# Weight blocks of a feed-forward pair dealt out in strict turn, with places of their own for the small ones

## The chip, the cores and the metric

One core of a Trainium2 chip runs the kernel. The metric is device time in microseconds (us), from the start to the end of one execution.

## The reference

A decoder trunk of two layers on 256 tokens of width 2048, all in 32-bit floats. Layer 0 has sparse attention with chosen keys, layer 1 a sliding window over shared keys and values; each is followed by a SwiGLU feed-forward part and a gated embedding. The change concerns the feed-forward part alone:

```python
def swiglu(h, w1, w3, w2):
    return (jax.nn.silu(h @ w1) * (h @ w3)) @ w2
...
        x = x + swiglu(rmsnorm(x, g_ffn[i]), w1[i], w3[i], w2[i])   # w1, w3: 2048 x 5632, w2: 5632 x 2048
```

## The kernel before

**Products in three parts.** Every 32-bit operand is split into a rounded part `hi` and a rest `lo`. A product of a 128x128 activation tile (the stationary side, `st_hi` and `st_lo`) with a 128x512 weight tile is three multiplications on PE (L379 to L381): `hi` by `st_hi`, `lo` by `st_hi`, `hi` by `st_lo`. The activations are split once, the weights as they stream in.

**The weight stream** (`WeightStream`) walks one list of blocks. A full block holds four weight tiles (1 MB, 128x2048) and feeds 24 multiplications: 4 tiles, 2 halves of the tokens, 3 parts. For each, the SP queue loads a place `raw` (3 places), ACT makes `hi` (L123) and DVE makes `lo` (L124) in a pool with 3 places each. `next()` hands the next block to PE, and splits ahead so far that the block in use and the two behind it are split (`LOOK`). A `hi` can be made only when PE is done with the block that held the place three blocks before. ACT, DVE, PE and the SP queue each work strictly in their order; a scheduler writes that order when the program is built.

**A pair of chunks.** The feed-forward part works on 11 pairs in each layer, each a 512-wide chunk of `w1` and the same chunk of `w3`, in groups of 3, 4 and 4; after a group its rows of `w2` follow as full blocks. A pair is 256 tokens by 2048 by twice 512. For the first 4 of its 16 weight tiles (two of each kind: quadrants B11, B21 of `w1` and B12, B22 of `w3`) the kernel uses a Strassen-like scheme of 7 products in place of 8: sums of quadrants against sums of activation quadrants (`s_hi`, `s_lo`), into `side` accumulators or straight into the four outputs `acc0` to `acc3` (c11, c21, c12, c22). These 7 blocks are small: two tiles, 128x1024, and 6 multiplications each. DVE forms the sums in place (L118). The other 12 tiles of each chunk come as 3 full blocks per chunk. So a pair has 7 small and 6 full blocks, 42 + 144 = 186 multiplications.

The list of a pair's blocks before is: r11, r12, F, r11, r21, F, r11, r22, F, r11, F, F, F, where an F is a full block and r11 is split anew after each sum. A small block takes one of the three full-size places for `hi` and `lo`, and counts as one block of look-ahead.

**The end of a pair.** DVE adds the side products into v1, v6, v7, v8 (L477 to L480) and the accumulators (L604, L610); ACT makes the sigmoid (L606) and DVE the gate u (L607, L611). The gate is turned: two DVE transposes of 32x32 blocks (L312) into `xb`, then 16 copies on ACT (L317, moves=(1, 1)) into `xt`, then a split into the station `hid` (L299 on ACT, L300 on DVE), which the products with `w2` read after the group.

Of the kernel before, what the change touches and what calls it, by code (L numbers as in the profile page):

```python
# [12 lines left out]
F32 = mybir.dt.float32  # L13
F32R = mybir.dt.float32r
# [4 lines left out]
P = 128  # L19
# [51 lines left out]
class Block:  # L71

    def __init__(self, src, a, n, held=None, loads=(), sums=()):
        self.src, self.a, self.n, self.held, self.loads, self.sums = src, a, n, held, loads, sums


class WeightStream:
# [6 lines left out]
    def __init__(self, tc, raw_pool, half_pool, blocks):  # L86
        self.tc, self.nc, self.raw_pool, self.half_pool = tc, tc.nc, raw_pool, half_pool
        self.blocks = blocks
        self.held_pool = None
        self.loaded, self.halves, self.held = {}, {}, {}  # L90
        self.n_loaded = self.n_split = self.at = 0
        self.after = None

    def load(self, pool=None):
        i = self.n_loaded
        if i >= len(self.blocks):
            return
        b = self.blocks[i]
        self.n_loaded += 1
        for name, src in b.loads:  # L100
            self.held[name] = t = self.held_pool.tile([P, b.a * b.n], F32, tag=name, name=name, bufs=1)
            self.nc.sync.dma_start(t.rearrange("p (a n) -> p a n", a=b.a), src)
# [9 lines left out]
    def split(self):  # L112
        i = self.n_split
        if i >= len(self.blocks):
            return
        b = self.blocks[i]
        for o, p in b.sums:
            self.nc.vector.tensor_add(self.held[o], self.held[o], self.held[p])  # L118
        raw = self.loaded.pop(i) if b.held is None else self.held[b.held]
        hi = self.half_pool.tile([P, 4 * CW], F32R, tag="hi", name="hi")  # L120
        lo = self.half_pool.tile([P, 4 * CW], F32R, tag="lo", name="lo")
        m = b.a * b.n
        done = (self.nc.scalar.activation(hi[:, :m], raw[:, :m], AF.Copy),  # L123
                self.nc.vector.tensor_sub(lo[:, :m], raw[:, :m], hi[:, :m].bitcast(F32)))  # L124
# [4 lines left out]
        self.n_split += 1  # L129
# [13 lines left out]
def yoco_kernel(  # L143
# [22 lines left out]
    def pair_cols(wa, ca, wb, cb, nk):  # L166

        def at(w, k, c):
            return w[k * P:(k + SN) * P, c:c + CW].rearrange("(a p) n -> p a n", p=P)

        b11, b21, b12, b22 = at(wa, 0, ca), at(wa, SN, ca), at(wb, 0, cb), at(wb, SN, cb)
        rest = [cols(w, 2 * SN, nk - 2 * SN, c, CW) for w, c in ((wa, ca), (wb, cb))]
        def held(name, **more):
            return Block(None, SN, CW, held=name, **more)
# [130 lines left out]
    def transposed_blocks(pool, src, out=None, bufs=1, moves=(0, 1)):  # L305


        xb = pool.tile([P, 4, 4, NT, 32], F32, tag="xb", name="xb", bufs=bufs)
        xt = (pool.tile([P, 4, S], F32, tag="xt", name="xt", bufs=2) if out is None else out).rearrange(
            "p k (t q) -> p k t q", t=NT)  # L310
        for t in range(NT):
            nc.vector.transpose(out=xb[:, :, :, t, :], in_=src[t].rearrange("p (k j f) -> p j k f", k=4, j=4))  # L312
        for i in range(4):
            for j in range(4):
                o, s = xt[32 * j:32 * j + 32, :, :, 32 * i:32 * i + 32], xb[32 * i:32 * i + 32, j]
                if moves[(i + j) % 2]:
                    nc.scalar.activation(o, s, AF.Copy)  # L317
# [32 lines left out]
    def square_sum(ss, c, scratch):  # L350
        for t in range(NT):
            sq = (ps_tr.tile([P, CW], F32, tag="tr", name="sq") if scratch is None
                  else scratch.tile([P, CW], F32, tag="g", name="sq", bufs=2))
            nc.scalar.activation(sq, x[t][:, c * CW:(c + 1) * CW], AF.Square, accum_out=ss[:, t, c:c + 1])

    def rstd_of(ss, name):
# [23 lines left out]
        nc.tensor.matmul(o, sh, l, start=False, stop=False)  # L380
        return nc.tensor.matmul(o, sl, h, start=False, stop=last)  # L381

    def accumulate(st, ktiles, n, acc, pace=(), start=0, end=None, new=None):


        block = 0
# [1 line left out]
        while done < (len(ktiles) if end is None else end):  # L388
            hi, lo, a = stream.next()
            for j in range(a):  # L390
# [1 line left out]
                h, l = hi[:, j * n:(j + 1) * n], lo[:, j * n:(j + 1) * n]  # L392
                first, last = done + j == (0 if new is None else start), done + j == len(ktiles) - 1
                for t in range(NT):
                    end_ = products(st, acc[t][:, :n], kt, t, h, l, first and (new is None or new[t]), last)
            done += a
            work(pace[block] if block < len(pace) else 0)
            block += 1
# [47 lines left out]
    def pair_of_chunks(st, forms, nk, quad):  # L446
# [8 lines left out]
        def form(o, of, alone):  # L455
            hi, lo, a = stream.next()
            for j in range(a):
                sl = slice(j * CW, (j + 1) * CW)
                products_of(*of(j), o, hi[:, sl], lo[:, sl], alone != "more" and j == 0, alone == "alone" and j == a - 1)
# [21 lines left out]
        form(c12, forms.of(4), "first")  # L481
        accumulate(st, ktiles, CW, (c12, c22), (), 2 * SN, 2 * SN + 4, new=(False, True))
        form(c21, tiles(SN, 1), "more")
        accumulate(st, ktiles, CW, (c11, c21), (), 2 * SN + 8)
# [111 lines left out]
    def feed_forward(layer, st, forms, r, ss, nxt, scratch):  # L596
        for gi, (f0, f1) in enumerate(FGROUPS):
            hid = new_station()
            for f in range(f0, f1):
                quad = [ps_acc.tile([P, CW], F32, tag="acc", name=f"acc{j}") for j in range(4)]  # L600
                v = pair_of_chunks(st, forms, KT, quad)
                u = []
                for t in range(NT):
                    nc.vector.tensor_add(v[t], v[t], quad[t])  # L604
                    u.append(scratch.tile([P, CW], F32, tag="g", name="u", bufs=2))
                    nc.scalar.activation(u[t], v[t], AF.Sigmoid, scale=r[:, t:t + 1])  # L606
                    nc.vector.scalar_tensor_tensor(u[t], v[t], r[:, t:t + 1], u[t], op0=ALU.mult, op1=ALU.mult)  # L607
                accumulate(st, ALL, CW, quad[2:], (), 2 * SN + 4)
                for t in range(NT):
                    nc.vector.tensor_sub(v[2 + t], quad[2 + t], v[2 + t])  # L610
                    nc.vector.scalar_tensor_tensor(u[t], v[2 + t], r[:, t:t + 1], u[t], op0=ALU.mult, op1=ALU.mult)  # L611
                ut = transposed_blocks(scratch, u, moves=(1, 1))
# [56 lines left out]
    def embedding_end(st, pst, r, ss, halves, scratch, emb_pool, end):  # L669
# [14 lines left out]
        for t in range(NT):  # L684
            for s in range(2):
# [7 lines left out]
                sq = scratch.tile([P, CW], F32, tag="g", name="sq", bufs=2)  # L693
# [246 lines left out]
```

## Time and profile before

| what | us |
|---|---|
| runs of the kernel before: median (lowest to highest of 3) | 2344.95 (2343.69 to 2347.48) |
| the profiled execution: its time | 2347.13 |
| its span, first to last instruction | 2345.4 |
| PE, DVE, ACT busy in the span | 2235.3, 1631.5, 1302.4 |
| the 22 pairs of chunks together | 1081.61 |

The profile is one execution, 2347.13 us long, of which 2345.4 us are its span. PE means the matrix engine, DVE the vector engine, ACT the scalar engine, POOL is hardly used, and SP issues nearly all loads. A line such as L123 is one of the kernel; `hi<-raw` is what it writes and reads. Behind a bar or in square brackets stands how long the engine was idle before, and who ended that. One thing needs care: a multiplication's record is longer than the spacing at which PE starts them, so records overlap, and PE's busy share hides waits. Starts have to be compared with starts.

### The profile page before, as it was taken

The numbers are of one execution on the slowest core, as the hardware profiler recorded it, in microseconds if no ns is written. First come the engines' busy times: TensorE is split into PE (matmuls) and PEld (weight loads), VectorE is DVE, ScalarE is ACT, GpSimd is POOL, SyncE is SP. The second block draws the span as 40 slices with busy tenths as digits, with TensorE's granted clock in tenths as the row PEclk, the third lists the DMA queues.
The fourth block names the chain that finished last, engine by engine and source line by source line (L and its number), as shares of the span: only waits on it lengthen the run. The fifth ranks groups of instructions, "written<-read, shape, count | busy, mean of one in ns | idle before, by whom it ended". The sixth has DMA issues, their size and how long they took to land.

```text
span 2345.4 us, 25010 instructions
## 1 busy us (share of the span) xinstructions
PE 2235.3 (95%) x9780; PEld 1793.8 (76%) x9780; DVE 1631.5 (70%) x1728; ACT 1302.4 (56%) x1698; POOL 39.1 (2%) x38
## 2 busy tenths in 40 slices
PE   9999999999899999999999999999999999999998
PEld 8787877777677877788788777777777787777877
DVE  5877776756776477767787777776577656777755
ACT  5556655543655355566675667555355633565653
POOL 0111000000000000000000000000000000000000
PEclk9999999999999999999999999999999999999999
DMA  7554645555446554465565455556554565445553
GB/s 247 180 180 144 215 149 174 192 185 163 164 151 223 182 167 159 145 214 195 169 225 198 149 175 170 174 174 201 168 182 160 188 197 176 156 153 198 200 184 123
DMA packets 211383, 419.23 MB, mean 179 GB/s; under 512 B 7729, under 2 KB 14513, under 8 KB 211137
## 3 DMA queue, kind: packets, MB, share of 16 engines
q1 hardware_dynamic: 208400, 410.68, 52.7%
q0 software_dynamic: 1248, 4.27, 0.6%
q10 hardware_dynamic: 1616, 2.69, 0.3%
q8 instruction: 76, 1.25, 0.2%
q14 instruction: 43, 0.34, 0.0%
HBM read 415.48 MB, written 2.12 MB: 178 GB/s over the span
## 4 chain that ended last, share of the span: by engine, by line
PE 78%; ACT 10%; DVE 9%; issue 2%; ACTq 0%; POOLq 0%; DVEq 0%; POOL 0%
PE acc L380 25%; PE acc L381 25%; PE acc L379 24%; DVE lo L124 5%; ACT hi L123 5%; ACT xt L317 4%; PE ps_s L537 1%; PE ps_o L574 1%; DVE v L477 1%; DVE v L610 0%; DVE u L611 0%; PE ps_p L565 0%; PE side L381 0%; PE side L380 0%; DVE xb L312 0%
## 5 line engine op out<-in xcount | busy, mean ns | idle before, releaser
L379 PE MATMUL acc<-hi,st_hi 128*128 128x512 f32 (+2 forms) x2872 | 1112.8, 392 | 43.7 <-ACT hi L123 43.3
L380 PE MATMUL acc<-lo,st_hi 128*128 128x512 f32 (+2 forms) x2872 | 1120.0, 390 | 32.4 <-DVE lo L124 32.4
L381 PE MATMUL acc<-hi,st_lo 128*128 128x512 f32 (+2 forms) x2872 | 1113.5, 388 | 0.0
L124 DVE TENSOR_TENSOR lo<-raw,hi 128x2048 fp32r<-128x2048 f32 (+1 forms) x347 | 793.0, 2291 | 394.3 <-ACT hi L123 393.1
L123 ACT ACTIVATE hi<-raw 128x2048 fp32r<-128x2048 f32 (+1 forms) x347 | 655.8, 1897 | 734.9 <-PE acc L381 640.3
L379 PEld LDWEIGHTS acc<-hi,st_hi 128*128 128x128 f32 x2872 | 540.3, 189 | 176.7 <-ACT hi L123 69.0
L380 PEld LDWEIGHTS acc<-lo,st_hi 128*128 128x128 f32 x2872 | 543.3, 189 | 154.4 <-DVE lo L124 48.1
L381 PEld LDWEIGHTS acc<-hi,st_lo 128*128 128x128 f32 x2872 | 543.1, 189 | 108.3 <-issue 2.0
L123 ACT ACTIVATE hi<-r 128x1024 fp32r<-128x1024 f32 x154 | 157.3, 1048 | 145.9 <-PE acc L381 82.1
L317 ACT ACTIVATE xt<-xb 32x256 f32<-32x256 f32 x544 | 225.7, 415 | 19.1 <-DVE xb L312 12.9
L124 DVE TENSOR_TENSOR lo<-r,hi 128x1024 fp32r<-128x1024 f32 x154 | 184.4, 1220 | 44.9 <-ACT hi L123 44.9
L118 DVE TENSOR_TENSOR r<-r,r 128x1024 f32<-128x1024 f32 x88 | 107.5, 1222 | 1.0
L300 DVE TENSOR_TENSOR st_lo<-xt,st_hi 128x1024 fp32r<-128x1024 f32 x30 | 36.7, 1223 | 55.3 <-ACT st_hi L299 55.3
L379 PE MATMUL side<-hi,s_hi 128*128 128x512 f32 x132 | 56.3, 426 | 9.9 <-ACT hi L123 9.8
L477 DVE TENSOR_TENSOR v<-v,side 128x512 f32<-128x512 f32 x22 | 15.2, 689 | 68.7 <-PE side L381 68.7
L319 DVE COPY xt<-xb 32x256 f32<-32x256 f32 x192 | 54.4, 283 | 2.4
L380 PE MATMUL side<-lo,s_hi 128*128 128x512 f32 x132 | 51.6, 391 | 1.5 <-DVE lo L124 1.5
L381 PE MATMUL side<-hi,s_lo 128*128 128x512 f32 x132 | 51.4, 389 | 0.0
L610 DVE TENSOR_TENSOR v<-acc,v 128x512 f32<-128x512 f32 x44 | 30.2, 692 | 27.9 <-PE acc L381 27.9
L621 DVE TENSOR_TENSOR x<-x,acc 128x512 f32<-128x512 f32 x48 | 32.8, 688 | 23.5 <-PE acc L381 23.5
L379 PEld LDWEIGHTS side<-hi,s_hi 128*128 128x128 f32 x132 | 24.7, 187 | 32.0 <-ACT hi L123 28.6
L551 ACT ACTIVATE sc<-sc,neg 128x128 f32<-128x128 f32 (+1 forms) x64 | 28.3, 444 | 31.3 <-DVE neg L549 31.3
(154 smaller groups left out, 1149.9 us busy)
## 6 DMA issues: line engine op xcount, KB each, us to landing
raw<-in_w_dram SPq DMA_DIRECT2D x220, 1024.0 KB, 5.2
r<-in_w_dram SPq DMA_DIRECT2D x88, 512.0 KB, 4.5
raw<-in_w_pg_dram SPq DMA_DIRECT2D x32, 1024.0 KB, 5.1
raw<-in_w_in_a_dram SPq DMA_DIRECT2D x24, 1024.0 KB, 5.2
raw<-in_w_out_a_dram SPq DMA_DIRECT2D x16, 1024.0 KB, 5.1
raw<-in_w_q_b_dram SPq DMA_DIRECT2D x16, 1024.0 KB, 5.1
raw<-in_w_out_b_dram SPq DMA_DIRECT2D x16, 1024.0 KB, 5.1
raw<-in_w_kv_dram SPq DMA_DIRECT2D x8, 1024.0 KB, 5.3
```

Of the source, the lines that this page charges most:

```text
L118: self.nc.vector.tensor_add(self.held[o], self.held[o], self.held[p])
L123: done = (self.nc.scalar.activation(hi[:, :m], raw[:, :m], AF.Copy), self.nc.vector.tensor_sub(lo[:, :m], raw[:, :m], hi[:, :m].bitcast(F32)))
L124: self.nc.vector.tensor_sub(lo[:, :m], raw[:, :m], hi[:, :m].bitcast(F32)))
L300: nc.vector.tensor_sub(lo, src, hi.bitcast(F32))
L317: nc.scalar.activation(o, s, AF.Copy)
L319: nc.vector.tensor_copy(o, s)
L379: nc.tensor.matmul(o, sh, h, start=first, stop=False)
L380: nc.tensor.matmul(o, sh, l, start=False, stop=False)
L381: return nc.tensor.matmul(o, sl, h, start=False, stop=last)
L477: nc.vector.tensor_add(v6, v1, p6)
L610: nc.vector.tensor_sub(v[2 + t], quad[2 + t], v[2 + t])
L621: nc.vector.tensor_add(xs, xs, acc[t])
```

## The change

- A pair's list has 12 blocks, small and full by turns: r11, F, r12, F, r11, F, R, F, r11, F, r11, F. B21 and B22 come in one place `r2` by two loads and are split as one block R of full size (12 multiplications).
- Small blocks have places of their own for their halves, `shi` and `slo`, one each, in the pool that also holds the quadrants. The look-ahead counts full blocks alone: three full ones and at most one small one are split ahead. The place for `r11` is doubled.
- The order of the products in a pair follows the list; the multiplications are the same 186. One accumulator, c21, now ends with a small block; one full block instead of two stands at the pair's end for c12 and c22.
- The gates are formed in place in v1, v7 and v6, v8; the sigmoid goes to a tile `sg`. The tiles with tag `g` (`sg`, and `sq` of the square sums) and the turned tile `xt` have one place instead of two.

```diff
     def split(self, i):
+        while self.n_loaded <= i + self.LOAD and self.n_loaded < len(self.blocks):
+            self.load()
...
+        if b.small:
+            pool, width, bufs, tag = self.held_pool, SN * CW, 1, "s"
+        else:
+            pool, width, bufs, tag = self.half_pool, 4 * CW, None, ""
+        hi = pool.tile([P, width], F32R, tag=tag + "hi", name=tag + "hi", bufs=bufs)
+        lo = pool.tile([P, width], F32R, tag=tag + "lo", name=tag + "lo", bufs=bufs)
...
     def next(self):
-        while self.n_split <= self.at + self.LOOK and self.n_split < len(self.blocks):
-            while self.n_loaded <= self.n_split + self.LOAD and self.n_loaded < len(self.blocks):
-                self.load()
-            self.split()
+        ahead = small = 0
+        for i in range(self.at, len(self.blocks)):
+            b = self.blocks[i]
+            if ahead > self.LOOK:
+                break
+            if i not in self.halves and not (b.small and small):
+                self.split(i)
+            if b.small:
+                small += 1
+            else:
+                ahead += 1
...
-        return [held("r11", loads=[("r11", b11)]),
-                held("r12", loads=[("r12", b12), ("r22", b22)], sums=[("r11", "r12"), ("r12", "r22")]), rest[0][0],
-                held("r11"), held("r21", loads=[("r21", b21)]), rest[0][1],
-                held("r11", sums=[("r11", "r22")]), held("r22"), rest[1][0],
-                held("r11", sums=[("r11", "r21")]), rest[0][2], rest[1][1], rest[1][2]]
+        return [held("r11", loads=[("r11", [b11])]), rest[0][0],
+                held("r12", loads=[("r12", [b12]), ("r2", [b21, b22])], sums=[("r11", "r12", 0), ("r12", "r2", 1)]),
+                rest[0][1], held("r11"), rest[1][0], held("r2", 2 * SN), rest[0][2],
+                held("r11", sums=[("r11", "r2", 1)]), rest[1][1], held("r11", sums=[("r11", "r2", 0)]), rest[1][2]]
...
-        xt = (pool.tile([P, 4, S], F32, tag="xt", name="xt", bufs=2) if out is None else out).rearrange(
+        xt = (pool.tile([P, 4, S], F32, tag="xt", name="xt", bufs=1) if out is None else out).rearrange(
...
-                  else scratch.tile([P, CW], F32, tag="g", name="sq", bufs=2))
+                  else scratch.tile([P, CW], F32, tag="g", name="sq", bufs=1))
...
-                    u.append(scratch.tile([P, CW], F32, tag="g", name="u", bufs=2))
-                    nc.scalar.activation(u[t], v[t], AF.Sigmoid, scale=r[:, t:t + 1])
-                    nc.vector.scalar_tensor_tensor(u[t], v[t], r[:, t:t + 1], u[t], op0=ALU.mult, op1=ALU.mult)
-                accumulate(st, ALL, CW, quad[2:], (), 2 * SN + 4)
+                    sg = scratch.tile([P, CW], F32, tag="g", name="sg", bufs=1)
+                    nc.scalar.activation(sg, v[t], AF.Sigmoid, scale=r[:, t:t + 1])
+                    nc.vector.scalar_tensor_tensor(v[t], v[t], r[:, t:t + 1], sg, op0=ALU.mult, op1=ALU.mult)
+                accumulate(st, ALL, CW, quad[2:], (), 2 * SN + 8)
```

Below, the blocks of a pair in the change are called S1, F1, S2, F2, S3, F3, R, F4, S4, F5, S5, F6 in the order of the list.

**PE, second pair of layer 0, the products with S2.** Before, at the pair's second full block `hi_3009`; `hi_3022` and `hi_3032` are small:

```order
L379 MATMUL acc0_2944<-hi_3009,st_hi_2107 128x512
L379 MATMUL acc1_2945<-hi_3009,st_hi_2107 128x512
L379 MATMUL side3_2950<-hi_3022,s_hi_2109 128x512
L379 MATMUL acc2_2946<-hi_3032,s_hi_2109 128x512
L380 MATMUL acc0_2944<-lo_3010,st_hi_2107 128x512
L381 MATMUL acc0_2944<-hi_3009,st_lo_2108 128x512
L380 MATMUL acc1_2945<-lo_3010,st_hi_2107 128x512
```

In the change, `hi_2874` is F2 and `shi_2973` is S2:

```order
L392 MATMUL acc0_2946<-lo_2875,st_hi_2107 128x512
L391 MATMUL side1_2953<-shi_2973,s_hi_2109 128x512
L393 MATMUL acc0_2946<-hi_2874,st_lo_2108 128x512
L391 MATMUL acc1_2947<-hi_2874,st_hi_2107 128x512
L392 MATMUL acc1_2947<-lo_2875,st_hi_2107 128x512
L393 MATMUL acc1_2947<-hi_2874,st_lo_2108 128x512
L391 MATMUL acc0_2946<-hi_2874,st_hi_2107 128x512
L392 MATMUL side1_2953<-slo_2974,s_hi_2109 128x512
L393 MATMUL side1_2953<-shi_2973,s_lo_2110 128x512
```

Before, a full block's first two multiplications were followed by first ones of the next two small blocks, ahead of its own `lo`. Now S2 stands inside F2: its first multiplication after 14 of F2's, its `lo` after 19; everything else in a pair is block after block, but for S3, whose first multiplication follows one of F3's and whose `lo` follows eleven.

**ACT at the start of the third pair of layer 0.** `xt` is the turned gate of the second pair. Before:

```order
L123 ACTIVATE hi_3284<-r11_3119 128x1024
L123 ACTIVATE hi_3294<-r21_3269 128x1024
L317 ACTIVATE xt_3236<-xb_3235 32x8x32 x16
L299 ACTIVATE st_hi_2629<-xt_3236 128x1024
L123 ACTIVATE hi_3322<-raw_3282 128x2048
L123 ACTIVATE hi_3335<-r11_3119 128x1024
L123 ACTIVATE hi_3345<-r22_3133 128x1024
```

In the change, `hi_3268` is F3, `shi_3281` is S2, `hi_3309` is R, `shi_3319` is S3, `hi_3349` is F4:

```order
L130 ACTIVATE hi_3268<-raw_3180 128x2048
L484 ACTIVATE v1_3262<-side0_3258 128x512
L329 ACTIVATE xt_3233<-xb_3232 32x8x32 x16
L130 ACTIVATE shi_3281<-r12_3130 128x1024
L311 ACTIVATE st_hi_2636<-xt_3233 128x1024
L130 ACTIVATE hi_3309<-r2_3132 128x2048
L130 ACTIVATE shi_3319<-r11_3098 128x1024
L130 ACTIVATE hi_3349<-raw_3266 128x2048
```

Two small halves stood ahead of the 16 copies before; now S2's half stands behind them, and the halves of R, S3 and F4 follow.

More of the change, by code (lines that the diff above doesn't have):

```diff
@@ L71, with __init__ @@
 class Block:
-    def __init__(self, src, a, n, held=None, loads=(), sums=()):
-        self.src, self.a, self.n, self.held, self.loads, self.sums = src, a, n, held, loads, sums
+    def __init__(self, src, a, n, held=None, loads=(), sums=(), unit=None):
+        self.src, self.a, self.n, self.held, self.loads, self.sums, self.unit = src, a, n, held, loads, sums, unit
+        self.small = held is not None and a == SN
 class WeightStream:
@@ L90, in __init__ @@
         self.loaded, self.halves, self.held = {}, {}, {}
-        self.n_loaded = self.n_split = self.at = 0
+        self.n_loaded = self.at = 0
         self.after = None
@@ L99, in load @@
         self.n_loaded += 1
-        for name, src in b.loads:
-            self.held[name] = t = self.held_pool.tile([P, b.a * b.n], F32, tag=name, name=name, bufs=1)
-            self.nc.sync.dma_start(t.rearrange("p (a n) -> p a n", a=b.a), src)
+        for name, srcs in b.loads:
+            self.held[b.unit, name] = t = self.held_pool.tile([P, len(srcs), SN * CW], F32, tag=name, name=name,
+                                                      bufs=2 if name == "r11" else 1)
+            for j, src in enumerate(srcs):
+                self.nc.sync.dma_start(t[:, j, :].rearrange("p (a n) -> p a n", a=SN), src)
         if b.held is not None:
@@ L110, in load, with split @@
         self.loaded[i] = t
[L112 to L115, printed above, removed]
+    def split(self, i):
+        while self.n_loaded <= i + self.LOAD and self.n_loaded < len(self.blocks):
+            self.load()
         b = self.blocks[i]
[L117 to L121, printed above, removed]
+        for o, p, j in b.sums:
+            o, p = self.held[b.unit, o][:, 0, :], self.held[b.unit, p][:, j, :]
+            self.nc.vector.tensor_add(o, o, p)
+        raw = self.loaded.pop(i) if b.held is None else self.held[b.unit, b.held].rearrange("p a n -> p (a n)")
+        if b.small:
[4 more added lines that the diff above has]
+        lo = pool.tile([P, width], F32R, tag=tag + "lo", name=tag + "lo", bufs=bufs)
         m = b.a * b.n
@@ L172, in pair_cols, with held @@
         rest = [cols(w, 2 * SN, nk - 2 * SN, c, CW) for w, c in ((wa, ca), (wb, cb))]
-        def held(name, **more):
-            return Block(None, SN, CW, held=name, **more)
-        return [held("r11", loads=[("r11", b11)]),
-                held("r12", loads=[("r12", b12), ("r22", b22)], sums=[("r11", "r12"), ("r12", "r22")]), rest[0][0],
-                held("r11"), held("r21", loads=[("r21", b21)]), rest[0][1],
-                held("r11", sums=[("r11", "r22")]), held("r22"), rest[1][0],
-                held("r11", sums=[("r11", "r21")]), rest[0][2], rest[1][1], rest[1][2]]
+        def held(name, a=SN, **more):
+            return Block(None, a, CW, held=name, unit=len(blocks), **more)
+        return [held("r11", loads=[("r11", [b11])]), rest[0][0],
+                held("r12", loads=[("r12", [b12]), ("r2", [b21, b22])], sums=[("r11", "r12", 0), ("r12", "r2", 1)]),
+                rest[0][1], held("r11"), rest[1][0], held("r2", 2 * SN), rest[0][2],
+                held("r11", sums=[("r11", "r2", 1)]), rest[1][1], held("r11", sums=[("r11", "r2", 0)]), rest[1][2]]
     IW = IDXN // 3
@@ L381, in products_of, with accumulate @@
         return nc.tensor.matmul(o, sl, h, start=False, stop=last)
-    def accumulate(st, ktiles, n, acc, pace=(), start=0, end=None, new=None):
+    def accumulate(st, ktiles, n, acc, pace=(), start=0, end=None, new=None, stop=(True, True)):
         block = 0
@@ L394, in accumulate @@
                 for t in range(NT):
-                    end_ = products(st, acc[t][:, :n], kt, t, h, l, first and (new is None or new[t]), last)
+                    end_ = products(st, acc[t][:, :n], kt, t, h, l, first and (new is None or new[t]), last and stop[t])
             done += a
@@ L453, in tiles, with form @@
             return lambda j: (st[0][:, k0 + j, sl], st[1][:, k0 + j, sl])
[L455 to L459, printed above, removed]
+        def form(o, of, alone, block=None, at=0):
+            hi, lo, _ = stream.next() if block is None else block
+            for j in range(SN):
+                sl = slice((at + j) * CW, (at + j + 1) * CW)
+                products_of(*of(j), o, hi[:, sl], lo[:, sl], alone in ("alone", "first") and j == 0,
+                            alone in ("alone", "last") and j == SN - 1)
         def side_acc(i):
@@ L470, in pair_of_chunks @@
         nc.scalar.activation(v1, p1, AF.Copy)
+        accumulate(st, ktiles, CW, (c11, c21), (), 2 * SN, 2 * SN + 4, new=(True, True))
         form(p7, forms.of(3), "alone")
-        accumulate(st, ktiles, CW, (c11, c21), (), 2 * SN, 2 * SN + 4, new=(True, True))
+        accumulate(st, ktiles, CW, (c11, c21), (), 2 * SN + 4, 2 * SN + 8)
         form(p5, forms.of(1), "alone")
-        form(c11, tiles(SN, 0), "more")
-        accumulate(st, ktiles, CW, (c11, c21), (), 2 * SN + 4, 2 * SN + 8)
+        accumulate(st, ktiles, CW, (c12, c22), (), 2 * SN, 2 * SN + 4, new=(True, True))
+        block = stream.next()
+        form(c11, tiles(SN, 0), "more", block)
+        form(c12, forms.of(4), "more", block, SN)
+        accumulate(st, ktiles, CW, (c11, c21), (), 2 * SN + 8, stop=(True, False))
         form(p6, forms.of(2), "alone")
@@ L480, in pair_of_chunks @@
         nc.vector.tensor_sub(v8, v7, p5)
[L481 to L484, printed above, removed]
+        accumulate(st, ktiles, CW, (c12, c22), (), 2 * SN + 4, 2 * SN + 8)
+        form(c21, tiles(SN, 1), "last")
         return v1, v7, v6, v8
@@ L692, in embedding_end @@
                 gated(emb_pool, acc[t][s][:, :H], emb[t][:, s * H:(s + 1) * H], r, t, c0, H)
[L693 removed]
+                sq = scratch.tile([P, CW], F32, tag="g", name="sq", bufs=1)
                 nc.scalar.activation(sq[:, :H], x[t][:, c0:c0 + H], AF.Square, accum_out=ss[:, t, c + s:c + s + 1])
@@ L773, in first_block @@
         stream.after = done
-        return stream.split()
+        return stream.split(0)
     stream.after = x_to_station(st, G_ATTN[0], 0, between=first_block)
```

6 lines of the change are left out of this document (2 added, 4 removed).

## The prediction

> **What bounds the kernel now.** I read the page's busy shares first, then a table of the six stretches that hold the 22 pairs, then PE's instructions in one pair, then those of ACT and DVE beside it.
>
> ```profile
> PE 2235.3 (95%) x9780; PEld 1793.8 (76%) x9780; DVE 1631.5 (70%) x1728; ACT 1302.4 (56%) x1698; POOL 39.1 (2%) x38
> ```
> ```profile
> 320.72:471.95 151.23, 136.49 (x560) 0.98 0.50 171
> 539.80:734.38 194.58, 178.66 (x746) 0.99 0.53 176
> 821.38:1016.37 194.99, 180.01 (x745) 0.98 0.49 165
> 1451.90:1600.30 148.40, 134.65 (x560) 0.99 0.52 174
> 1668.13:1864.37 196.24, 180.28 (x746) 0.98 0.52 175
> 1951.33:2147.50 196.17, 180.21 (x745) 0.98 0.49 164
> sum 1081.61, PE 990.30; mean PE 165.05
> ...
> 734.38:821.38 87.00, 87.00 (x385) 1.00 0.57 186
> 399.87:403.28 3.41, 3.41 (x10) 0.50 0.96 326
> ```
>
> Columns of the table: stretch, length, PE busy, granted clock, DMA share, GB/s. The stretch from 734.38 is products with w2: 4 chunks of 4 full blocks, 384 multiplications in 87.00 us, one per 0.2266 us, with no wait. That is PE's own pace, with the loads kept up at 186 GB/s. At it the pairs need 22 x 186 x 0.2266 = 927.3 us. They take 1081.61: 154.3 us are lost there, 7.0 a pair. (By busy time it would be 1081.61 - 990.30 = 91.3; the records overlap, so the pace of starts decides.) The clock column sums, (1 - clock) x length, to 18 us; a half-clock stretch of 3.41 us like the last row costs 1.7, so there are some ten. The rest, 136, is waiting. Where, the second pair shows:
>
> ```profile
> 371.78 0.39 PE L381 MATMUL acc<-hi,st_lo 128*128 128x512 f32 x1
> 372.01 0.39 PE L379 MATMUL side<-hi,st_hi 128*128 128x512 f32 x1
> ...
> 374.50 0.39 PE L381 MATMUL side<-hi,s_lo 128*128 128x512 f32 x1
> 374.73 0.61 PE L379 MATMUL acc<-hi,st_hi 128*128 128x512 f32 x2
> 375.66 0.50 PE L379 MATMUL side<-hi,s_hi 128*128 128x512 f32 x1 [0.31 <-ACT hi L123]
> 377.66 0.50 PE L380 MATMUL acc<-lo,st_hi 128*128 128x512 f32 x1 [1.50 <-DVE lo L124]
> 378.00 0.40 PE L381 MATMUL acc<-hi,st_lo 128*128 128x512 f32 x1
> ...
> 385.05 0.39 PE L381 MATMUL acc<-hi,st_lo 128*128 128x512 f32 x1
> ...
> 388.53 0.50 PE L380 MATMUL acc<-lo,st_hi 128*128 128x512 f32 x1
> ...
> 395.71 0.39 PE L381 MATMUL acc<-hi,s_lo 128*128 128x512 f32 x1
> 395.94 0.64 PE L379 MATMUL acc<-hi,st_hi 128*128 128x512 f32 x2
> 396.78 0.50 PE L379 MATMUL acc<-hi,st_hi 128*128 128x512 f32 x1 [0.21 <-ACT hi L123]
> 398.58 0.50 PE L379 MATMUL acc<-hi,st_hi 128*128 128x512 f32 x1 [1.30 <-ACT hi L123]
> ...
> 422.82 0.39 PE L379 MATMUL side<-hi,st_hi 128*128 128x512 f32 x1
> ```
>
> This pair runs from 372.01 to 422.82, 50.8 us, where its pace needs 42.15. From 374.50 to 377.66 four starts take 3.16 us in place of 0.91: 2.25 lost, plus 0.11 on the slow restart (0.34 to the next start). From 385.05 to 388.53, five starts, it is 2.35 in pieces, from 395.71 to 398.58 1.96, and at 399.87 a half-clock stretch follows. The waits end with a `hi` or `lo`: PE waits for weights that are loaded, but not yet split. They come just after small blocks, which occupy full-size places and one step each of look-ahead, though PE is through with one in 6 x 0.2266 = 1.36 us.
>
> **The change, part by part.** I walk one steady pair of the new list, each engine in its order, with these durations:
>
> ```profile
> 372.26 1.92 ACT L123 ACTIVATE hi<-raw 128x2048 fp32r<-128x2048 f32 x1 [3.55 <-PE acc L381]
> 374.55 1.99 ACT L123 ACTIVATE hi<-r 128x1024 fp32r<-128x1024 f32 x2
> 376.45 6.81 ACT L317 ACTIVATE xt<-xb 32x256 f32<-32x256 f32 x16
> 383.29 1.06 ACT L299 ACTIVATE st_hi<-xt 128x1024 fp32r<-128x1024 f32 x1
> 384.26 1.90 ACT L123 ACTIVATE hi<-raw 128x2048 fp32r<-128x2048 f32 x1
> ...
> 413.10 1.32 ACT L606 ACTIVATE u<-v,r_ffn 128x512 f32<-128x512 f32 x2
> ```
> ```profile
> 371.53 1.37 DVE L610 TENSOR_TENSOR v<-acc,v 128x512 f32<-128x512 f32 x2 [1.56 <-PE acc L381]
> 372.82 1.41 DVE L611 SCALAR_TENSOR_TENSOR u<-v,r_ffn,u 128x512 f32<-128x512 f32 x2
> 374.14 1.30 DVE L312 STREAM_TRANSPOSE xb<-u 128x512 f32<-128x512 f32 x2
> 375.36 2.25 DVE L124 TENSOR_TENSOR lo<-raw,hi 128x2048 fp32r<-128x2048 f32 x1
> 377.53 2.35 DVE L124 TENSOR_TENSOR lo<-r,hi 128x1024 fp32r<-128x1024 f32 x2
> 379.80 1.22 DVE L118 TENSOR_TENSOR r<-r,r 128x1024 f32<-128x1024 f32 x1
> ```
>
> Time 0 is the start of the last multiplication of the pair before (here 371.78), so PE could start S1 at 0.23. An engine that waits for PE starts 0.48 after the last start (372.26), one that waits for ACT 0.05 after its end; work in a row starts about 0.1 before the end of the one before.
> - DVE finishes the turned gate at 3.66 (375.44), as now. ACT makes F3's `hi` at 0.48 to 2.4, then v1, then the 16 copies from 3.7: 6.8 us, to 10.5. Only behind them comes S2's `hi`: 10.4 to 11.5. Its sums (two of 1.22 behind F3's `lo`) are ready at 8.2, so the copies decide.
> - PE reaches the first product with S2 after S1, F1 and 14 of F2: 0.23 + 44 x 0.2266 = 10.2. **It waits till 11.55: 1.35, and 0.1 for the restart.** S2's `lo` (11.5 to 12.75) is there before its product at 13.0.
> - PE is through S2 at 13.9 and F2 at 15.05. ACT: `st_hi` to 12.4, R to 14.25, S3 14.4 to 15.45, F4 15.5 to 17.4. DVE: `st_lo`, R to 16.6, S3 to 17.75, F4 to 19.9. PE wants S3's `hi` at 15.5 and its `lo` at 18.0, R at 22.1, F4 at 24.8. S3 arrives on the dot.
> - Then there is room: S4, behind a sum, is split by 23.4 and wanted at 30.2. F5's `hi` needs F3's place (22.3), its `lo` ends at 26.6, wanted at 31.6.
> - The late half is DVE's: v6 waits for S4's product (31.8), then the next pair's F1 (to 34.7), v7, S5's `lo` (to 36.5), wanted at 37.0: 0.5 to spare. After it v6, v8, v1, v7, the next F2 (39.25 to 41.5), the gate, and the next S1 by 43.35, wanted at 43.85.
>
> So a pair lasts 42.15 + 1.45 = 43.6 in place of 50.8. Such pairs, following another one, are 16 of 22. The 4 first pairs of later groups have no copies ahead of S2, since products with w2 precede them: 0. The 2 first of a layer stand behind the turning of x; no row has their order, so between 0 and all they lose now, and I take the 1.45 of their nearest kin, since it too is copies ahead of S2.
>
> Half-clock stretches: some ten follow about 60 waits (three a pair, as above) of around 2 us, in pieces. For 18 waits of 1.45 I take one in ten, 2 x 1.7 = 3.4; bounds 0 and 18 x 1.7 = 31. The Trainium skill, "TensorE: Matmul & The Clock Gate", HAM oscillation, asks for an idle gap of more than about 3.4 us before PE is slowed. By that no wait here would do it, and the time would be 3.4 lower; but the trace disagrees, since the stretch at 399.87 follows waits that sum to 2.0.
>
> The small edits. DVE needs per pair about 7 x 2.25 + 5 x 1.18 + 4 x 1.22 + 12 operations of v and gate at 0.7 + 1.3 + 1.2 = 37.5 us, ACT some 28, both under PE's 42.15; R saves one start on each (1.99 to 1.9 on ACT, 2.35 to 2.25 on DVE), covered by PE. One place for `sg` makes the second sigmoid wait for the first gate: ACT ends at 42.9, its next work for PE starts at 44.1, so 0; with that cover gone, 0.7 a pair. One place for `xt` and `sq`: their users come once per chunk of 16 or more tiles, 20 us apart; 0, at most the 6.8 of copies once per group. Gates in place: 0, the same operations.
>
> Loads and the SP queue: r2 has one place, free when its second sum is done (24.6). Its two loads stand on SP ahead of F2's and F3's raw loads of the next pair.
>
> ```profile
> DMA to landing us min/median/max: 4.4/5.2/10.1
> ```
>
> The place for F2's raw data is free at 26.7 (F5's `lo`), so it lands at 32 to 37 and is wanted at 37.3. r12 (freed at 12.75), r2 and r11 are needed after 49. The rate rises to 8.4 MB in 43.6 us, 192 GB/s, as in the w2 stretch. Hidden: 0.
>
> Sum: lost now 154.3; lost then 18 x 1.45 + 3.4 = 29.5; gain 124.8. From the profiled 2347.1 (span 2345.4 and 1.7 around it) that gives 2222; the median of the runs shown is 2.2 lower, so **2220**.
>
> **The rivals.**
> - *Every S2 wait brings a half-clock stretch*: 16 more x 1.7 = 27 us, 2247. For it: 1.96 did once. Against: most waits of about 2 now do not. 0.12.
> - *DVE becomes the bound of the late half.* The 0.5 to spare are small against its 37.5 us of work; 2 us lost a pair give 16 x 2 = 32, 2252. 0.13.
> - *The waits only change places*: `hi` still waits for three full-size places. Half the loss stays: 77 - 29 = 48 more, 2268. Against: in the walk each full block has 2 us or more to spare. 0.08.
> - *The wait for S2 vanishes*, if the copies start earlier: 16 x 1.45 = 23 less, 2197. 0.05.
> - *Slower: SP held up by r2.* If F2's raw data land later than 37.3, 10.7 us after the place is free, each microsecond costs 16. Beyond about 18.5 us the gain is gone; at 20 us, 16 x 9.3 = 149, 2369. Against: the longest landing in the trace is 10.1. 0.03.
>
> **How the numbers follow.** The first case has the other 0.59. The range reaches from the case without the S2 wait to between DVE's case and that of moved waits: 2195 to 2262; left out are the slow case, most of moved waits, and tails. The likeliest case alone: 2205 to 2235. A measurement here tells 0.2%, 5 us, from no change. Faster 0.96, same 0.01, slower 0.03: all cases but the last are far on one side.
>
> **What would show it.** Right: pairs 43.6 apart (copies of v1 on ACT), one wait of about 1.4 in each pair that follows another, on `side` with S2, released by ACT; nothing at F3 to F6; first pairs of later groups 42.2 long; the waits for `lo` of L124 gone. Wrong: PE waiting for `slo` or a full `lo` late in a pair (DVE), clock at 0.5 after every S2 (the first rival), ACT waiting for data (loads).

## The result and the profile after

The changed kernel takes **2230.23 us** (median of 4 runs, 2229.68 to 2230.67) where the kernel before took 2344.48 (4 runs, 2343.69 to 2347.48): a ratio of 0.951, with a 95% interval of 0.9494 to 0.9527. The forecast was 2220 with a range of 2195 to 2262. The profiled execution took 2229.82 us, its span 2228.0.

The first line of the page, then PE's two largest groups and the one that waits longest (a group is the products of one line into one kind of tile; behind the bar stand busy time, mean ns, and idle time with what ended it):

```profile
PE 2178.8 (98%) x9780; PEld 1787.4 (80%) x9780; DVE 1627.3 (73%) x1706; ACT 1315.1 (59%) x1676; POOL 39.1 (2%) x38
```
```profile
L391 PE MATMUL acc<-hi,st_hi 128*128 128x512 f32 (+2 forms) x2828 | 1092.8, 387 | 3.3 <-ACT hi L130 3.3
L392 PE MATMUL acc<-lo,st_hi 128*128 128x512 f32 (+2 forms) x2828 | 1091.2, 386 | 2.7 <-DVE lo L131 2.6
...
L391 PE MATMUL side<-shi,s_hi 128*128 128x512 f32 x132 | 54.3, 412 | 30.1 <-ACT shi L130 30.1
```

Before, the same products into `acc`, from full blocks in the main, had waited 43.3 us for a weight's `hi` (and 0.4 for a `st_hi`) and 32.4 us for a `lo`:

```profile
L380 PE MATMUL acc<-lo,st_hi 128*128 128x512 f32 (+2 forms) x2872 | 1120.0, 390 | 32.4 <-DVE lo L124 32.4
...
L379 PE MATMUL acc<-hi,st_hi 128*128 128x512 f32 (+2 forms) x2872 | 1112.8, 392 | 43.7 <-ACT hi L123 43.3 <-ACT st_hi L299 0.4
```

Now 3.3 and 2.7 are left, all of it outside the 22 pairs. Within them one kind of wait stands alone: products with a small block's sum (`side` from `shi` and `s_hi`) wait for ACT. The list of waits counts it (us in total, times, longest):

```profile
PE side L391 <- ACT shi L130: 30.1, 18, 1.8
```

Eighteen waits in 22 pairs. A table of five pairs, each from the last start of the pair before to its own last start, says in which (start and end, length, busy time of each engine, granted clock, DMA share, GB/s):

```profile
320.40:364.12 43.72, 42.46 (x187) 34.83 (x186) 34.71 (x37) 28.94 (x33) 0.72 (x1) 1.00 0.59 196
364.12:408.54 44.42, 42.60 (x187) 34.75 (x186) 36.26 (x32) 27.94 (x32) 0.00 (x0) 1.00 0.57 189
782.01:824.17 42.16, 42.16 (x187) 34.91 (x186) 29.87 (x24) 19.99 (x15) 0.00 (x0) 1.00 0.61 203
606.51:650.74 44.23, 42.52 (x187) 34.76 (x186) 36.15 (x32) 27.88 (x32) 0.00 (x0) 1.00 0.57 191
650.74:694.97 44.23, 42.52 (x187) 34.76 (x186) 36.15 (x32) 27.88 (x32) 0.00 (x0) 1.00 0.57 191
```

The first pair of a layer lasts 43.72, the second 44.42, a first pair of the third group 42.16 (PE's pace, nothing lost), and each further pair 44.23. The first pair of the second group begins among products with w2: from 466.06 to 562.28, where it ends, 425 starts take 96.2 us, which is PE's pace too, and so it is in layer 1. Against 42.16 that loses 2 x 1.56 + 2 x 2.26 + 14 x 2.07 = 36.6 us, where 154.3 were lost before. The difference, 117.7, is the difference of the spans, 2345.4 - 2228.0 = 117.4, to 0.3 us: the gain lies in the pairs. The clock stands at 1.00 in every row, and in the other pairs too: no half-clock stretch is left in them.

Now one such pair on PE. Starts are the first column:

```profile
606.51 0.39 PE L393 MATMUL acc<-hi,st_lo 128*128 128x512 f32 x1
606.74 0.39 PE L391 MATMUL side<-shi,st_hi 128*128 128x512 f32 x1
...
616.48 0.39 PE L392 MATMUL acc<-lo,st_hi 128*128 128x512 f32 x1
618.58 0.50 PE L391 MATMUL side<-shi,s_hi 128*128 128x512 f32 x1 [1.71 <-ACT shi L130]
618.92 0.40 PE L393 MATMUL acc<-hi,st_lo 128*128 128x512 f32 x1
...
650.97 0.39 PE L391 MATMUL side<-shi,st_hi 128*128 128x512 f32 x1
```

From 616.48 to 618.58 one start takes 2.10 in place of 0.23: 1.87 lost. It is the first product with S2, as forecast. ACT and DVE at the same time:

```profile
606.94 1.92 ACT L130 ACTIVATE hi<-raw 128x2048 fp32r<-128x2048 f32 x1 [1.12 <-PE acc L393]
608.80 0.60 ACT L484 ACTIVATE v<-side 128x512 f32<-128x512 f32 x1
610.62 6.83 ACT L329 ACTIVATE xt<-xb 32x256 f32<-32x256 f32 x16 [1.22 <-DVE xb L324]
617.47 1.06 ACT L130 ACTIVATE shi<-r 128x1024 fp32r<-128x1024 f32 x1
```
```profile
602.10 2.29 DVE L131 TENSOR_TENSOR lo<-raw,hi 128x2048 fp32r<-128x2048 f32 x1
604.30 0.75 DVE L622 SCALAR_TENSOR_TENSOR v<-v,r_ffn,sg 128x512 f32<-128x512 f32 x1
604.97 1.22 DVE L131 TENSOR_TENSOR slo<-r,shi 128x1024 fp32r<-128x1024 f32 x1
606.10 0.75 DVE L622 SCALAR_TENSOR_TENSOR v<-v,r_ffn,sg 128x512 f32<-128x512 f32 x1
606.76 1.28 DVE L625 TENSOR_TENSOR v<-acc,v 128x512 f32<-128x512 f32 x2
607.96 1.41 DVE L626 SCALAR_TENSOR_TENSOR v<-v,r_ffn,v 128x512 f32<-128x512 f32 x2
609.28 1.31 DVE L324 STREAM_TRANSPOSE xb<-v 128x512 f32<-128x512 f32 x2
```

Read upward from the wait: S2's `hi` (617.47) stands behind the 16 copies, which begin at 610.62 as the transposes end at 610.59; ACT had idled 1.22 for them. The transposes end DVE's row without a gap: the next pair's F2 (602.10), the gate of v1, the next S1, the gate of v7, then the subtraction at 606.76, though PE's last start was at 606.51.

### The profile page after: what moved, and what is told of

It is laid out like the page before. It is cut to its first block, busy times and chain, and to the rows that moved or that the text cites. A ratio compares the mean times of both kernels' runs of the same rounds, so it can differ in the third digit from the quotient of the medians.

```text
span 2228.0 us, 24973 instructions
## 1 busy us (share of the span) xinstructions
PE 2178.8 (98%) x9780; PEld 1787.4 (80%) x9780; DVE 1627.3 (73%) x1706; ACT 1315.1 (59%) x1676; POOL 39.1 (2%) x38
## 4 chain that ended last, share of the span: by engine, by line
PE 78%; ACT 10%; DVE 9%; issue 3%; DVEq 0%; POOLq 0%; POOL 0%; ACTq 0%
PE acc L393 23%; PE acc L392 23%; PE acc L391 23%; ACT xt L329 5%; DVE lo L131 2%; ACT hi L130 2%; PE side L391 2%; PE side L392 1%; PE side L393 1%; DVE v L626 1%; DVE v L622 1%; PE ps_s L553 1%; DVE slo L131 1%; DVE v L625 1%; PE ps_o L590 1%
## 5 line engine op out<-in xcount | busy, mean ns | idle before, releaser
L392 PE MATMUL acc<-lo,st_hi 128*128 128x512 f32 (+2 forms) x2828 | 1091.2, 386 | 2.7 <-DVE lo L131 2.6
L131 DVE TENSOR_TENSOR slo<-r,shi 128x1024 fp32r<-128x1024 f32 x110 | 134.3, 1221 | 83.9 <-ACT shi L130 83.8
L130 ACT ACTIVATE shi<-r 128x1024 fp32r<-128x1024 f32 x110 | 115.7, 1052 | 71.0 <-DVE r L121 59.9
L391 PE MATMUL side<-shi,s_hi 128*128 128x512 f32 x132 | 54.3, 412 | 30.1 <-ACT shi L130 30.1
L131 DVE TENSOR_TENSOR lo<-r,hi 128x2048 fp32r<-128x2048 f32 x22 | 50.4, 2292 | 18.8 <-ACT hi L130 18.8
L391 PEld LDWEIGHTS side<-shi,s_hi 128*128 128x128 f32 x132 | 24.7, 187 | 45.0 <-ACT shi L130 41.1
L392 PE MATMUL side<-slo,s_hi 128*128 128x512 f32 x132 | 51.4, 389 | 0.0
L393 PE MATMUL side<-shi,s_lo 128*128 128x512 f32 x132 | 51.3, 389 | 0.0
L621 ACT ACTIVATE sg<-v,r_ffn 128x512 f32<-128x512 f32 x44 | 31.5, 717 | 31.4 <-DVE v L622 31.3
L130 ACT ACTIVATE hi<-r 128x2048 fp32r<-128x2048 f32 x22 | 41.9, 1905 | 12.0 <-PE acc L393 12.0
```

Source lines behind the costliest of these rows:

```text
L391: nc.tensor.matmul(o, sh, h, start=first, stop=False)
L621: nc.scalar.activation(sg, v[t], AF.Sigmoid, scale=r[:, t:t + 1])
```

## The experiments

Two theories on the gain. A: the strict turn carries it, so that it stays when the small halves go back to full-size places. B: the places and the look-ahead carry it, whatever the list. The later experiments ask about what is left: whether it is the turning of the gate that S2 waits for, and what ends that wait. In their edits `tc_order(tc, one, before)` puts the instruction `one` behind `before`.

**1. Turn kept, old places** (`e1_turn_old_places`)

```diff
-        if b.small:
-            pool, width, bufs, tag = self.held_pool, SN * CW, 1, "s"
-        else:
-            pool, width, bufs, tag = self.half_pool, 4 * CW, None, ""
+        pool, width, bufs, tag = self.half_pool, 4 * CW, None, ""
...
-            if i not in self.halves and not (b.small and small):
+            if i not in self.halves:
                 self.split(i)
-            if b.small:
-                small += 1
-            else:
-                ahead += 1
+            ahead += 1
```

> The changed kernel with its list of blocks kept (small and full by turns, R as one), but small blocks split into the three full-size places and counted by the look-ahead, as before. Theory A (the turn does it): in strict turn a block's place is always released one full and one small block before it is wanted, 5.44 + 1.36 = 6.8 us, and a split needs at most 4.2, so the time stays within 20 us of the changed kernel's 2230: 2225 to 2250. Theory B (small blocks in full-size places are the trouble): half or more of the 114 us comes back, 2290 or more.

Measured: 2342.34 us (2340.26 to 2344.56), ratio 0.9973 (0.9948 to 0.9999). Nearly the whole gain is gone, so A falls. Two pairs, a following one and a first one of a group, then PE and ACT in the former:

```profile
576.02:627.23 51.21, 44.99 (x188) 35.91 (x187) 36.19 (x32) 27.78 (x32) 0.00 (x0) 0.93 0.53 164
817.23:859.39 42.16, 42.16 (x188) 34.92 (x187) 30.30 (x25) 20.34 (x15) 0.00 (x0) 1.00 0.62 200
```
```profile
582.72 0.39 PE L387 MATMUL acc<-hi,st_lo 128*128 128x512 f32 x1
588.82 0.80 PE L385 MATMUL side<-hi,s_hi 128*128 128x512 f32 x1 [5.72 <-ACT hi L127]
```
```profile
580.89 6.80 ACT L323 ACTIVATE xt<-xb 32x256 f32<-32x256 f32 x16 [1.22 <-DVE xb L318]
587.71 1.06 ACT L127 ACTIVATE hi<-r 128x1024 fp32r<-128x1024 f32 x1
```

Without copies at its head the pair runs at full pace (42.16). With them, PE has S1 and F1, 30 x 0.2266 = 6.8 us, and then stands 5.72 till the copies and S2's `hi` are through. The third place is S2's, and F2, which would cover the wait, is not split. F2 gets the place of S1, whose last product started at 577.28, so the place was soon free; but on ACT F2's `hi` stands behind S2's and starts at 589.62 only. The edit changes the places and the look-ahead together; which of the two costs more isn't shown.

**2. Old list, new places** (`e2_old_list_new_places`): the changed kernel (`shi` and `slo`, the new look-ahead, the small edits) with the list of before; `r2` is loaded as one but split as two small blocks:

```diff
+        return [held("r11", loads=[("r11", [b11])]),
+                held("r12", loads=[("r12", [b12]), ("r2", [b21, b22])], sums=[("r11", "r12", 0), ("r12", "r2", 1)]), rest[0][0],
+                held("r11"), held("r2", at=0), rest[0][1],
+                held("r11", sums=[("r11", "r2", 1)]), held("r2", at=1), rest[1][0],
+                held("r11", sums=[("r11", "r2", 0)]), rest[0][2], rest[1][1], rest[1][2]]
```

> The changed kernel with small halves in places of their own and full blocks alone counted, but with the list of before (small blocks two in a row, two full blocks at the end, B21 and B22 as two small blocks). Theory A (the turn): the second of two small blocks in a row waits for the product of the first, then for its hi and lo, up to 2.5 us three times a pair, less what other blocks fill: 2280 to 2345. Theory B (the places): near the changed kernel, 2225 to 2250.

Measured: 2350.53 us (2349.5 to 2352.58), ratio 1.0001 (0.9974 to 1.0027). B falls too. A following pair, its first three waits, and what ACT does before the first:

```profile
585.20:635.00 49.80, 44.98 (x188) 35.65 (x187) 36.27 (x33) 27.70 (x33) 0.00 (x0) 0.97 0.52 169
```
```profile
596.74 0.50 PE L394 MATMUL side<-shi,s_hi 128*128 128x512 f32 x1 [1.59 <-ACT shi L132]
600.56 0.51 PE L394 MATMUL acc<-shi,st_hi 128*128 128x512 f32 x1 [0.70 <-ACT shi L132]
603.61 0.79 PE L395 MATMUL acc<-slo,st_hi 128*128 128x512 f32 x1 [2.54 <-DVE slo L133]
```
```profile
588.78 6.83 ACT L332 ACTIVATE xt<-xb 32x256 f32<-32x256 f32 x16
595.63 1.06 ACT L132 ACTIVATE shi<-r 128x1024 fp32r<-128x1024 f32 x1
```

All three end with a small half, but not for one reason. The first `hi` stands behind the 16 copies, like S2's in the change; its place was free 2 us before, since PE's last product with the small block ahead of it started at 593.15. The other two belong to the next small block. It needs the same place: its `hi` starts at 599.45, as PE is through with the block before (last start at 599.02), and its `lo` at 602.34, behind the `lo` of a full block that fills DVE from 600.13.

Together: neither part alone gains more than a few microseconds, both together 114. That the three times lie so close is in part chance. The granted clock is 0.977 over the span of experiment 1 and 0.980 in 2, against 0.991 before and 0.999 in the change, so that (1 - clock) x span is 54 and 47 us against 21 and 2. With that taken off each span, experiment 1 would lie some 40 us below the kernel before and experiment 2 some 24; this is an estimate, and too high, since PE also waits in such stretches. By it each part alone saves something, which the half clock takes back. While ACT copies the gate, PE needs some ten microseconds of blocks already split. Three full blocks give that (16 us). Here it took places of their own for the small ones together with a list that never asks for two small ones in a row; two small places with the old list, or more full-size places, were not tried.

**3. B21 and B22 apart** (`e3_r_apart`): the change, with R as two small blocks

```diff
-                rest[0][1], held("r11"), rest[1][0], held("r2", 2 * SN), rest[0][2],
+                rest[0][1], held("r11"), rest[1][0], held("r2", at=0), held("r2", at=1), rest[0][2],
```

> The changed kernel, but B21 and B22 split as two small blocks one behind the other, in the one small place, where R stood. Theory A: r22 waits for r21's product and its own split, at most 2.5 us in each of 22 pairs, 55 us: 2235 to 2285. If one block for both is only a matter of one start less on ACT and DVE: 2230.

Measured: 2242.04 us (2241.76 to 2242.31), ratio 0.9527 to before (0.9425 to 0.9628), 11.8 us above the change. So the joint block is worth about a tenth of the gain. The time lies in the range of theory A, but by luck: no product waits for r22. Following pairs last 44.61, 2.45 above PE's pace. Of this 1.75 is still the wait for S2 (18 waits, at most 1.6); the rest is restarts and starts that come late by 0.1 us or less, and what makes them late isn't shown.

```profile
607.89:652.50 44.61, 43.02 (x188) 34.34 (x187) 36.07 (x33) 28.14 (x33) 0.00 (x0) 1.00 0.58 189
```
```profile
PE side L393 <- ACT shi L132: 28.1, 18, 1.6
```

**4. The small edits alone** (`e4_small_edits_on_before`): the kernel before, with gates in place and one place for `sg`, `sq` and `xt`

```diff
-        xt = (pool.tile([P, 4, S], F32, tag="xt", name="xt", bufs=2) if out is None else out).rearrange(
+        xt = (pool.tile([P, 4, S], F32, tag="xt", name="xt", bufs=1) if out is None else out).rearrange(
...
-                    nc.vector.scalar_tensor_tensor(u[t], v[t], r[:, t:t + 1], u[t], op0=ALU.mult, op1=ALU.mult)
+                    nc.vector.scalar_tensor_tensor(v[t], v[t], r[:, t:t + 1], sg, op0=ALU.mult, op1=ALU.mult)
```

> The kernel before with the small edits alone: gates formed in place, one place instead of two for sg, sq and xt. Prediction's step: they cost nothing and bring nothing, 2344.5, within 5. If one place for sg or xt delays the turned gate, up to 0.7 us a pair, 2360; if in-place gates shorten DVE's chain, below 2339.

Measured: 2353.65 us, ratio 1.0018 (0.9971 to 1.0065): no difference that could be told, though the median lies outside the 5 us given. Its runs spread from 2343.05 to 2374.06, and the granted clock goes with them, from 0.993 down to 0.975. In the profiled execution (2372.04, clock 0.976) PE's waits sum to 92.7 us, no more than the 100.9 before; what is longer there is the half clock. From 7 us faster to 15 slower stays open.

**5. The gate first on DVE** (`e5_gate_first_on_dve`): the change, with the next F2's `lo` and S2's sums ordered behind the transposes (`one` is each of the two sums, `first` the `lo` of the next pair's F2)

```diff
+            if len(b.sums) == 2 and self.turned is not None:
+                tc_order(self.tc, one, self.turned)
...
+        if first is not None:
+            tc_order(tc, first, turned)
```

> The changed kernel, with DVE's order at a pair's end altered: the lo of the next pair's F2 and the sums for S2 stand behind the transposes of the gate instead of ahead of it. The scheduler then also puts S2's product behind all of F2 on PE, and R's hi ahead of S2's on ACT. Theory (the gate was late since DVE worked through F2's lo first): the transposes end 3.7 us after the start of the pair's last multiplication, not 4.08 as in the changed kernel. Rival (they wait for PE's last product as before): 4.1 stays. The pair still waits for S2, 1.9 by the walk (S2's hi ends at 14.3, wanted at 12.5): 2225 to 2235.

Measured: 2235.21 us (2235.11 to 2235.31), 5 more than the change and 0.2 above the range given. The transposes did come earlier (the last start of the pair before was at 607.17), but look at what ACT does next:

```profile
609.52 1.30 DVE L329 STREAM_TRANSPOSE xb<-v 128x512 f32<-128x512 f32 x2
```
```profile
610.86 6.83 ACT L337 ACTIVATE xt<-xb 32x256 f32<-32x256 f32 x16 [0.86 <-DVE xb L329]
617.72 1.92 ACT L134 ACTIVATE hi<-r 128x2048 fp32r<-128x2048 f32 x1
619.54 1.04 ACT L316 ACTIVATE st_hi<-xt 128x1024 fp32r<-128x1024 f32 x1
620.48 1.04 ACT L134 ACTIVATE shi<-r 128x1024 fp32r<-128x1024 f32 x1
```
```profile
621.57 0.50 PE L399 MATMUL side<-shi,s_hi 128*128 128x512 f32 x1 [1.78 <-ACT shi L134]
```

The transposes end at 3.65 after that last start, in place of 4.08. But the scheduler, given S2's sums later, put R's `hi` and the turned gate's `st_hi` ahead of S2's `hi`: 2.8 us between the copies and S2. The gain was made and given away at once.

**6. S2 and S3 one block later on PE** (`e6_s2_s3_one_block_later`): the products with S2 stand behind F2, those with S3 behind F3

```diff
-        form(p7, forms.of(3), "alone")
+        block = stream.next()
         accumulate(st, ktiles, CW, (c11, c21), (), 2 * SN + 4, 2 * SN + 8)
-        form(p5, forms.of(1), "alone")
+        form(p7, forms.of(3), "alone", block)
+        block = stream.next()
         accumulate(st, ktiles, CW, (c12, c22), (), 2 * SN, 2 * SN + 4, new=(True, True))
+        form(p5, forms.of(1), "alone", block)
```

> The changed kernel, with the products of S2 and S3 put behind the full block that follows them on PE (F2, F3); order of loads and splits on ACT and DVE unchanged but for F4's halves ahead of S3's. Theory (PE waits for S2 alone, and S2's half is ready at 12.0, its lo at 13.3): the wait shrinks from 1.87 to about 0.6, S3 adds 0.2: 2210 to 2218. Rival (ACT's 16 copies delay everything behind them alike, the wait moves to R or F4): 2230.

Measured: 2210.93 us (2210.59 to 2211.11), ratio 0.9424 to before (0.941 to 0.9438). The waits for S2's `hi` are gone; in their place the 16 following pairs wait half a microsecond for its `lo`:

```profile
PE side L392 <- DVE slo L131: 8.0, 16, 0.6
```

**7. The copies cut in two** (`e7_copies_cut`): 10 copies, then S2's `hi`, then the other 6; R's halves behind S3's (`behind` is S2's `hi`, `r` is `i + 2`)

```diff
+CUT = 10
...
+                        if behind is not None and n > CUT:
+                            tc_order(tc, one, behind)
...
+        if b.small and r in self.done and self.blocks[r].held == "r2":
+            for one, before in zip(self.done[r], done):
+                tc_order(self.tc, one, before)
```

> The changed kernel, with ACT's 16 copies of the turned gate cut in two: 10, then S2's hi, then 6; and R's halves behind S3's. Theory (S2's hi waits only for the copies ahead of it): ready at 9.7, wanted at 10.0, no wait there; S3 then waits some 0.5: 2200 to 2210. Rival (the sums for S2 on DVE are what is late): the wait stays above 1, 2220 or more.

Measured: 2210.00 us (2209.43 to 2210.25), ratio 0.942 (0.9404 to 0.9436). No work was removed, only its order on ACT and DVE changed, and the wait for S2 is gone from the following pairs; so it was the copies ahead of its `hi` that held PE there. The waits that are left are S3's, behind the last six copies and `st_hi`, and the two of S2 in the first pairs of layers, where the copies of x stand ahead:

```profile
PE side L406 <- ACT shi L132: 7.8, 18, 1.3
```

**8. Both** (`e8_cut_and_later`)

> Both: copies cut (10 and 6 around S2's hi, R behind S3) and the products of S2 and S3 one full block later. Theory: no wait is left in a pair that follows another; each lasts 42.2 us: 2230 less 16 x 2.0 = 2198, 2193 to 2205. Rival (DVE has no time left, its late half goes over PE's pace as its cover shrinks): 2210 or more, with waits for slo or lo late in the pair.

Measured: **2193.12 us** (2193.07 to 2193.19), ratio 0.9348 to before (0.9335 to 0.9362). This beats the change by 37 us. Every kind of pair (first and second of a layer, following one, first of a group) lasts PE's pace:

```profile
320.55:362.71 42.16, 42.16 (x188) 34.91 (x187) 34.53 (x37) 28.70 (x33) 0.72 (x1) 1.00 0.61 204
362.71:404.87 42.16, 42.16 (x188) 34.91 (x187) 36.23 (x32) 27.83 (x32) 0.00 (x0) 1.00 0.58 198
598.68:640.84 42.16, 42.16 (x188) 34.91 (x187) 36.11 (x32) 27.77 (x32) 0.00 (x0) 1.00 0.59 200
770.03:812.19 42.16, 42.16 (x188) 34.91 (x187) 29.59 (x24) 19.88 (x15) 0.00 (x0) 1.00 0.60 204
```

The 36.6 us counted as lost in the change are what came back: 2230.2 - 36.6 = 2193.6.

**9. The gate first on DVE, S2 next on ACT** (`e9_gate_first_s2_next_on_act`): experiment 5 with ACT's order kept: R's halves behind S2's, and `st_hi` behind S2's `hi` (`behind`)

```diff
+        if b.held == "r2" and i - 4 in self.done:
+            for one, before in zip(done, self.done[i - 4]):
+                tc_order(self.tc, one, before)
...
+                    one, _ = split(hid[0][sl], hid[1][sl], ut)
+                    if behind is not None:
+                        tc_order(tc, one, behind)
```

> The change, with F2's lo and S2's sums behind the gate's transposes on DVE, as in e5; on ACT, S2's hi now stands right behind the 16 copies, ahead of the turned gate's st_hi and of R's hi, as in the change itself. On PE the first product with S2 then stands after 20 of F2's products (14 in the change). Theory: the transposes end 3.65 after the last start of the pair before, as in e5, the copies at 10.5, S2's hi at 11.5; PE reaches its first product at 0.23 + 50 x 0.2266 = 11.56, so a following pair loses at most 0.2 in place of 2.07: 2230.2 - 16 x 1.9 = 2200, range 2196 to 2206. Rival: S2's hi comes no earlier than in the change (its wait is set by something beside the turn); then only the 6 products more, 1.36 us, cover, a wait of 0.5 and a restart of 0.1 stay: 2230.2 - 16 x 1.46 = 2207. If the 2235 of e5 came from the later lo of F2 and not from S2's place on ACT: about 2230 or more.

Measured: 2203.21 us (2202.87 to 2203.32), ratio 0.9384 (0.9351 to 0.9417). In a pair whose last start before it was at 600.52:

```profile
602.88 1.30 DVE L332 STREAM_TRANSPOSE xb<-v 128x512 f32<-128x512 f32 x2
```
```profile
604.21 6.83 ACT L340 ACTIVATE xt<-xb 32x256 f32<-32x256 f32 x16 [0.86 <-DVE xb L332]
611.07 1.06 ACT L134 ACTIVATE shi<-r 128x1024 fp32r<-128x1024 f32 x1
```

Transposes to 3.66, copies to 10.52, S2's `hi` to 11.61. In the change these were 4.08, 10.94 and 12.02. PE, with 6 more products ahead, then loses 0.45 a pair (42.61 - 42.16), some 0.25 more than expected, and the time is inside the range given (start and end, length, busy times, clock, DMA share, GB/s):

```profile
600.52:643.13 42.61, 42.61 (x187) 34.68 (x186) 36.33 (x32) 27.36 (x32) 0.00 (x0) 1.00 0.57 198
```

What 5 lost was S2's place on ACT.

## Why the prediction was right, and which step was off

- **The place of the gain.** Right: the waits of the two groups into `acc` fell from 76.1 to 6.0 us, and none is left at F3 to F6 in any of the 22 pairs.
- **The wait that stays.** Right in place (the first product with S2), in engine (ACT, behind the 16 copies) and in which pairs: 16 following ones, and 2 that are first in a layer. The latter lose 1.56 where 1.45 was taken, which is luck: PE wants S2 there after 9 of F2's products, not 14, and on ACT eight copies and four scaled ones of x stand ahead in place of the 16. First pairs of later groups lose nothing, as forecast.
- **Its size: the term that was too small.** A wait of 1.35 and 0.1 for the restart was forecast, with pairs of 43.6; 1.87 and 0.2 came, with pairs of 44.23. The step behind it reads "DVE finishes the turned gate at 3.66, as now". It was carried over from before, while the same walk, at its other end, filled DVE to the end of the pair ("the gate, and the next S1 by 43.35") and put only one of the two gates there. The second, 606.10 to 606.85, pushes the subtraction (606.76) past PE's last start (606.51), where before it began 0.25 ahead of it; the transposes end 4.08 after that start. That makes 0.42 of the 0.52 missing; the other 0.1 is that S2's `hi` starts at the copies' end and not 0.1 before it. Experiment 9 gives DVE the free hands that the step assumed, and gets 3.66 and 10.52, the numbers of the walk.
- **Half-clock stretches.** 3.4 us were taken, none came. The bounds (0 and 31) held, the rate of one in ten did not. By pairs, the profile before has a half-clock stretch in 10 of 22, and in 7 of the 16 following ones, whose waits are alike; that gave no rate for one wait of another length.
- **The sum.** 36.6 lost in place of 29.5 makes 7.1 of the 10.2 that the forecast was low. Two errors partly cancel in it, which is luck: the waits cost 10.5 more than the 26.1 taken, the half clock 3.4 less. Another 2.6 is the place of the profiled execution among the runs: before it stood 2.2 above its median, after 0.4 below.
- **Small edits, R, loads.** The small edits at 0: experiment 4, on the kernel before, finds no difference within 0.3% faster and 0.65% slower; in the changed kernel they weren't tried apart. R was costed as covered; that held, and experiment 3 shows that the joint block is worth 11.8 us, which the prediction hadn't set apart. Loads hidden: 191 GB/s in a following pair, as the 192 worked out, and PE waits for ACT and never for data there.
- **Rivals.** Half clock after every wait: refuted by the clock of 1.00. DVE as the bound of the late half: no late wait for a `lo`; but DVE's full row showed at the other end, as the 0.42. Waits that change places: refuted for the change; experiment 2 shows such a move, to the one small place. The wait that vanishes: not in the change, but in experiment 8 at 2193, by another way than the earlier copies of the forecast. Slower by late loads: refuted by the time.

## What to carry to other kernels

Count look-ahead in the time that the blocks keep PE busy, not in blocks: small blocks that take a place and a step each starved PE here, and neither places of their own nor a better order helped alone. When two changes each bring nothing, look at the clock too, since part of what one of them saves may have gone into half-clock stretches. When a walk of a queue is used to place its next work, carry the end of the walk over to its beginning; a start time taken from the old profile holds only if that engine is as free as it was. And after an order is changed by hand, look at what the scheduler put into the gap, for it can cost as much as was gained.

## What the runs showed of the hardware

Half-clock stretches don't go by the length of a single wait. Before, where no wait of PE's was above 1.5 us but several stood in each pair, 10 pairs of 22 had one. In the change 18 waits of up to 1.8 us, one a pair, left the clock at 1.00. In experiment 2 waits of 1.59, 0.70 and 2.54 within 7 us brought a mean of 0.97 over the pair (the last two came with a single product between them), and in experiment 1 one of 5.72 with a short one behind it 0.93. In experiment 5, where a wait of about 1.9 stood in each following pair, one pair alone was slowed, to 46.14 us and a clock of 0.96; the pair behind it lasted 44.5, and its twin in layer 0, with the same loss of 2.03 at S2, 44.6 at full clock:

```profile
1438.89:1485.03 46.14, 44.28 (x187) 35.86 (x187) 36.99 (x33) 27.60 (x32) 0.00 (x0) 0.96 0.54 183
```

The Trainium skill, "TensorE: Matmul & The Clock Gate", HAM oscillation, names idle gaps of more than about 3.4 us. Experiment 1 agrees with it (5.72), and so does the change (1.8, no slowing); the kernel before and experiments 2 and 5 don't, with no wait above 1.5, 2.6 and 1.9. What exactly is counted stays open.
